# Attention's pieces planned with latencies that depend on the solve, and their end announced three jobs ahead

## The chip, the cores and the metric

One core of one Trainium2 chip runs the whole program. The metric is the device time of one execution in microseconds (us), the median over runs; for the kernel before it is 903.2 us over three runs (903.09 to 905.04).

## The reference

One layer of a hybrid block over 512 positions of 1024 channels, in fp32. After an RMSNorm, one projection `w_in` gives q, k, v of a stick-breaking attention, r, k, v and low-rank parts of an RWKV-7 branch, and two gates per channel:

```
h = rmsnorm(x, attn_norm_g);  proj = h @ w_in
# attention, 8 heads of 64, strictly causal, blocks of 128 queries
z = q @ k.T / 8;  keep = log_sigmoid(-z) where s < t else 0
w = exp(log_sigmoid(z) + sum of keep over s < j < t);  o_sb = w @ v
# RWKV-7, 8 heads of 64
S_t = S_(t-1) diag(w_t) + (S_(t-1) a_t) b_t^T + v_t k_t^T;  y_t = S_t r_t
o_rw = (groupnorm(y) + bonus) * gate
m = sigmoid(gate_0) * (o_sb @ w_branch_0) + sigmoid(gate_1) * (o_rw @ w_branch_1)
x = x + m @ w_out
u = causal_conv3(rmsnorm(x) @ w_ffn_up);  x = x + (silu(u_gate) * u_val) @ w_ffn_down
```

## The kernel before

Activations lie with channels on the 128 partitions and the 512 positions along the free axis. Every large product is made of three matmuls per 128 x 128 weight tile (weight high part times activation high and low part, weight low part times activation high part), so one output tile of `w_in` (8 weight tiles, called a dense tile here) is 24 matmuls of 512 columns. The weights of a tile come by a DMA on SP's queue (`load_w`, line 106, tile `wraw`, two buffers); ScalarE casts the high part (`whi`, line 108), and the low part (`wlo`) is made by ScalarE or VectorE with an accumulating DMA on POOL's queue (line 126).

After a short first stage the kernel has one long stage, which this change is about, and then the stages of the gates, `w_branch`, `w_out`, `w_up` and `w_down`, which run one dense product after another on TensorE (tiles `pf`, lines 138 to 140). In the long stage six streams of work are written as Python generators and merged by a planner, `interleave`, which runs when the program is built:

- `rw_stream(p)`, p = 0 to 3: RWKV for one pair of heads. Preparation, transposes and masked products (`st1`, lines 559 and 564), then the solve of small triangular systems: 31 steps of two VectorE operations (lines 595 and 597), whose result goes out and back through DRAM by DMAs on SP's queue (`su` and `st`, lines 602 and 604, then `U1` and `TT`, lines 608 and 611). The first matmul that reads it is line 618. After lines 629 to 649 comes a loop over 8 chunks (lines 666 to 691), the group norm and the output gate (line 715).
- `att_stream(p)`, the four chained: attention for one pair of heads, called a piece here. After the norms of q and k (lines 161 and 162) and the transposes of v (line 757) it has eight jobs, `(h, j)` with j from 3 down to 0 for each of two heads. A job works on n = 512 - 128 j columns: `scores` (TensorE lines 772 to 774 into a bank `pz`; then Abs, Exp, Ln on ScalarE, line 779 on VectorE, and the split into `sph`, `spl`; on POOL, lines 787 to 790, the running sum `ach`, `acl` that the next job reads), `weights` (lines 802 and 805 add onto the same `pz`, two Exps on ScalarE make `wth` and `w`, VectorE makes `wtl`) and `values` (lines 821 and 822). `pz` has two banks, so the scores of a job wait for the Exps of the job two before it.
- `dense_stream`: the dense tiles of q, k, v, r, k, v of all pairs (line 925, tiles `pd`) and, as filler, 13 of the 16 gate tiles (`NGATE`). Which tile comes next is decided in `pick`: r, k, v of the next RWKV pair first, then q, k, v of the next attention piece, each only once the event it hangs on (`prep`, `core`) is planned to come within `LAT["ahead"]` = 11059 ns; a gate tile otherwise.

Each stream yields its work in ns of TensorE time and its waits: `("lat", ns)` keeps it off the engine for so long, `("after", event)` until an event, `("set", event, ns)` announces one. The planner keeps a clock and takes at each point a stream that is ready. So the latencies, in the table `LAT`, set how far apart the steps of a stream stand in the instruction order; they wait for nothing on the chip. A piece is planned by `att0` and `att1`: job j may have its weights planned `att0[p] + att1[p] * (4 - j)` ns after its scores, and the event `core{p}`, on which q, k and v of the next piece hang, is set behind the piece's last values. The order of the instructions on the engines follows the planner, moved a little by the framework's own scheduling.

Where the long stage ends, TensorE goes on to three gate tiles, which need nothing of attention or RWKV (`pf`, first matmul line 138), and then to `w_branch`.

Of the kernel before, what the change touches and what calls it, by code (L numbers as in the profile page):

```python
# [52 lines left out]
def hybrid_block(ctx: ExitStack, tc: tile.TileContext, xT, w_in, vecs, decay_up, iclr_up, out_gate_up,  # L53
# [24 lines left out]
    def f(ap):  # L78
        return ap.bitcast(F32)
# [51 lines left out]
    def split(hi, lo, src):  # L131
        A.copy(hi, src)  # L132
        V.tensor_tensor(lo, src, f(hi), op=ALU.subtract)
# [20 lines left out]
    def f32r_pair(pool, tag):  # L154
        if tag == "wt":
            return tuple(pool.tile([P, T], F32R, tag=tag, name=tag + x, bufs=2) for x in "hl")
        return tuple(pool.tile([P, T], F32R, tag=tag + x, name=tag + x) for x in "hl")
# [26 lines left out]
    gl0 = f32r_pair(cpool, "gl0")  # L184
    gl1 = cpool.tile([96, T], F32R, name="gl1")
# [229 lines left out]
    def rbank():  # L415
        return bank(psr, "pr")
# [40 lines left out]
    def rw_stream(p):  # L457
        d = RD[p]
        yield ("after", f"prep{p - 1}")
        if p == 0:  # L460
            yield ("lat", LAT["rw0"][p])


        sic = []
        for j, bn in ((0, "db"), (1, "ib")):
# [11 lines left out]
            sic.append(e)  # L477
            yield (427, LAT["lup"][p] if j or p else 0)
        s, ic = sic
# [15 lines left out]
        V.tensor_tensor(sl, kk, f(sh), op=ALU.subtract)  # L495
        yield ("lat", LAT["sq"][p])
        pn = rbank()
# [39 lines left out]
        split(rh, rl, k)  # L537
        yield ("lat", LAT["prep"][p])
        pb = rbank()
# [10 lines left out]
        for hf in range(2):  # L550
            QA = rwp.tile([P, 4, 2, 256], F32, tag="QA", name="QA", bufs=4)
            QAs.append(QA)
            for c2 in range(2):
# [16 lines left out]
                for h in range(2):  # L570
                    A.copy(QA[:, 2 * c2 : 2 * c2 + 2, h].rearrange("p j (s n) -> p j s n", s=4)[:, :, 0:4:3],
                           pp[h][:, 256:512].rearrange("p (j s n) -> p j s n", j=2, s=2))
                yield (1400, LAT["st1"][p])
            for h, (hr, ho) in enumerate(HROWS):
# [17 lines left out]
        for q in range(31):  # L592
            n, m = 31 - q, q // 4 + 1
# [8 lines left out]
        nc.sync.dma_start(su.rearrange("b q (k g) t -> g (b q) k t", g=4), U)  # L602
        for g in range(4):
            nc.sync.dma_start(st[:, :, g], ut[32 * g : 32 * g + 16])
        yield ("lat", LAT["solve"][p])
        yield ("after", f"back{p - 1}")
        for h, (hr, _) in enumerate(HROWS):
# [115 lines left out]
    def att_stream(p):  # L723
# [42 lines left out]
        jobs = [(h, j) for h in range(2) for j in range(3, -1, -1)]  # L766
        st = {}

        def scores(h, j):
            n = T - P * j  # L770
            z = bank(psz, "pz")
            PE.matmul(z[:, 0:n], k2[h][:, j * P : (j + 1) * P], q2[h][:, j * P : T], start=True, stop=False)
            PE.matmul(z[:, 0:n], klo[h][:, j * P : (j + 1) * P], q2[h][:, j * P : T], start=False, stop=True)
            PE.matmul(z[:, 0:P], idb, mskb, start=False, stop=True, skip_group_check=True)
            e = atp.tile([P, T], F32, tag="e", name="e", bufs=3)
            act(e[:, 0:n], z[:, 0:n], AF.Abs)
            act(e[:, 0:n], e[:, 0:n], AF.Exp, scale=-1.0)
            act(e[:, 0:n], e[:, 0:n], AF.Ln, bias=1.0)
            V.scalar_tensor_tensor(e[:, 0:n], z[:, 0:n], 0.0, e[:, 0:n], op0=ALU.max, op1=ALU.add)
            sp = [atp.tile([P, n if j % 2 else T], F32R, tag=f"sp{x}{j if j % 2 else 0}", name=f"sp{x}{j}")[:, 0:n]  # L780
                  for x in "hl"]
            split(*sp, e[:, 0:n])

            if j == 3:
                ac = sp
            elif j > 0:
                G.tensor_tensor(e[:, P:n], e[:, P:n], st[h, j + 1]["e"][:, 0 : n - P], op=ALU.add)
                ac = [atp.tile([P, 3 * P], F32R, tag=f"ac{x}", name=f"ac{x}")[:, 0:n] for x in "hl"]
                G.tensor_copy(ac[0], e[:, 0:n])
                G.tensor_tensor(ac[1], e[:, 0:n], f(ac[0]), op=ALU.subtract)  # L790
            else:
                ac = None
            st[h, j] = dict(z=z, sp=sp, ac=ac, e=e)
            return n * 0.84 + 60

        def weights(h, j):
            n = T - P * j
            z, sp = st[h, j]["z"], st[h, j]["sp"]
            cost = 0
            if j < 3:  # L800
                for part in st[h, j + 1]["ac"]:
                    PE.matmul(z[:, P:n], none_, part, start=False, stop=True, skip_group_check=True)
                    cost += max(60, (n - P) * 0.42)
            for part in sp:
                PE.matmul(z[:, 0:n], ntri, part, start=False, stop=True, skip_group_check=True)  # L805
                cost += max(60, n * 0.42)
            w = atp.tile([P, T], F32, tag="e", name="w", bufs=3)
            wh, wl = f32r_pair(atp, "wt")
            act(wh[:, 0:n], z[:, 0:n], AF.Exp)
            act(w[:, 0:n], z[:, 0:n], AF.Exp)  # L810
            V.tensor_tensor(wl[:, 0:n], w[:, 0:n], f(wh[:, 0:n]), op=ALU.subtract)
            st[h, j]["w"] = wh, wl
            return cost

        def values(h, j):
            hr, ho = HROWS[h]
            n = T - P * j
            if j == 3:
                st[h, "po"] = bank(pso, "po")
            po, (wh, wl) = st[h, "po"], st[h, j]["w"]  # L820
            PE.matmul(po[:, j * P : T], vt[h][:, j], wh[:, 0:n], start=(j == 3), stop=False, skip_group_check=True)
            PE.matmul(po[:, j * P : T], vt[h][:, j], wl[:, 0:n], start=False, stop=(j == 0), skip_group_check=True)
            if j == 0:
                if h == 0:
                    st["ot"] = atp.tile([P, T], F32, tag="q0", name="ot")
                ot = st["ot"]
                A.copy(ot[hr], po[ho])
                V.tensor_tensor(ot[hr], ot[hr], po[hr], op=ALU.add)
            return 2 * n * 0.42

        def lat(j):
            return LAT["att0"][p] + LAT["att1"][p] * (4 - j)

        ready, free = {}, 0.0
        for i in range(-1, len(jobs)):
            if i + 1 < len(jobs):
                yield ("lat", max(0.0, free - clock["now"]))
                cost = scores(*jobs[i + 1])
                ready[i + 1] = clock["now"] + cost + lat(jobs[i + 1][1])
                yield (cost, 0)  # L840
            if i >= 0:
                yield ("lat", max(0.0, ready[i] - clock["now"]))
                cost = weights(*jobs[i])
                if i > 0:
                    cost += values(*jobs[i - 1])
                free = clock["now"] + cost + LAT["w"][p]
                yield (cost, 0)
        yield ("lat", LAT["val"][p])
        cost = values(*jobs[-1])
        A.dma_start(o_sb[p], st["ot"])  # L850
        yield ("set", f"core{p}")
        yield (cost, 0)

    clock = {"now": 0.0, "events": {f"{n}-1": 0.0 for n in ("prep", "core", "back")}}
    clock["events"]["back-2"] = 0.0
    gates = {}

# [16 lines left out]
    def dense_stream():  # L874
# [12 lines left out]
        def pick():  # L887
            for q in (rwq, atq):
                if q and all(ev.get(e, 1e12) <= clock["now"] + LAT["ahead"] for e in q[0][4]):
                    return q.pop(0)  # L890
            if gq and (rwq or atq or 16 - len(gq) < NGATE):
                return gq.pop(0)
# [12 lines left out]
        while cur:  # L905
# [14 lines left out]
            else:  # L920
# [10 lines left out]
            i += 1  # L931

    NGATE = 13
    FULL, SHORT = 0.65, 450
    LAT = dict(evac=5520, ahead=11059, k0=12000, gl0=1, gl1=2, att0=(1332, 762, 1125, 1575),
               att1=(810, 810, 810, 688), gn=(659, 3062, 2114, 3270), hop=(1073, 1254, 767, 762),
               lup=(8543, 2168, 5055, 862), pl=(671, 2115, 609, 2223), prep=(9000, 9000, 9000, 9000),
               pu=(1860, 2060, 1022, 1951), qk=(1409, 1644, 4330, 575), rw0=(5400, 1679, 2305, 1342),
               solve=(46500, 49755, 50000, 50000), sq=(2447, 1872, 3786, 557), sq_a=(1958, 1741, 1565, 328),
# [52 lines left out]
    def chain(*gens):  # L992
        for g in gens:
            yield from g

    interleave([rw_stream(p) for p in range(4)] + [chain(*(att_stream(p) for p in range(4))), dense_stream()])
    ph1.close()
    state["dma"] = False
# [147 lines left out]
```

## Time and profile before

| | us |
|---|---|
| median of 3 runs | 903.2 |
| the profiled execution, its own time | 898.13 |
| its span, first to last instruction | 896.4 |
| TensorE with matmuls, share of the span | 859.0 (96%) |
| VectorE, ScalarE, POOL busy | 562.5, 503.5, 148.1 |
| mean granted clock of TensorE | 0.987 |

The profile has one row per group of instructions with its busy time, and a trace of every instruction with start, duration and what released its engine after an idle time. The granted clock is 1.0 at TensorE's 2.4 GHz and 0.5 at 1.2 GHz. Ends of matmuls are modelled, so one matmul's duration is longer than the distance to the next.

### The profile page before, as it was taken

How to read it: one execution, taken by the hardware profiler on the slowest of the kernel's cores; microseconds unless marked ns; L12 is line 12 of the kernel's file. 1: busy time of each engine (PE TensorE's matmuls, PEld its weight loads, DVE VectorE, ACT ScalarE, POOL GpSimd, SP SyncE). 2: the span in 40 equal slices, each digit the busy share in tenths (PEclk: the TensorE clock that was granted, in tenths of full speed). 3: DMA queues.
4: the chain of work that ended last, by engine and by line, in shares of the span. 5: the costliest groups of instructions: out<-in, count | busy, mean ns of one | idle time of the engine just before them, and what ended most of it. 6: DMA issues, size and time to landing. Idle time of an engine off the chain costs nothing.

```text
span 896.4 us, 12726 instructions
## 1 busy us (share of the span) xinstructions
PE 859.0 (96%) x4598; PEld 676.7 (75%) x4598; DVE 562.5 (63%) x1138; ACT 503.5 (56%) x886; POOL 148.1 (17%) x214
## 2 busy tenths in 40 slices
PE   7889999988999989799999999999999999999998
PEld 4667767766777768586788878888888888888886
DVE  7669896894578681346666557777777777532222
ACT  7777988875766755677654454444444444321120
POOL 4633523251312523132000000000000000000000
PEclk9999999998899999899999999999999999999999
DMA  9476567338457548643664433333333333333431
GB/s 261 78 152 146 114 129 136 78 63 192 99 118 148 124 106 168 125 102 99 207 192 130 141 106 94 99 102 104 96 94 94 95 94 96 94 123 100 129 100 42
DMA packets 175151, 106.94 MB, mean 119 GB/s; under 512 B 29584, under 2 KB 156688, under 8 KB 175088
## 3 DMA queue, kind: packets, MB, share of 16 engines
q1 hardware_dynamic: 161408, 81.61, 32.3%
q0 software_dynamic: 10656, 19.40, 12.9%
q10 hardware_dynamic: 3024, 5.11, 1.6%
q8 instruction: 36, 0.59, 0.3%
q14 instruction: 27, 0.22, 0.1%
HBM read 78.31 MB, written 8.39 MB: 97 GB/s over the span
## 4 chain that ended last, share of the span: by engine, by line
PE 77%; DMA 7%; DVE 5%; ACT 5%; issue 2%; POOL 2%; SPq 1%; ACTq 0%; POOLq 0%; DVEq 0%
PE pf L138 17%; PE pf L139 17%; PE pf L140 17%; PE pd L925 13%; DMA wraw<-in_w_in 4%; PE pr L675 1%; PE pr L564 1%; DMA wlo<-wraw 1%; DMA U<-st 1%; PE pz L805 1%; DVE tm L595 1%; DVE U L597 1%; PE pr L559 1%; ACT whi L108 1%; PE pr L649 1%
## 5 line engine op out<-in xcount | busy, mean ns | idle before, releaser
L108 ACT CAST whi<-wraw 128x1024 fp32r<-128x1024 f32 (+1 forms) x131 | 129.1, 985 | 179.2 <-PE pf L139 146.9
L128 DVE TENSOR_TENSOR wlo<-wraw,whi 128x512 fp32r<-128x512 f32 (+1 forms) x178 | 114.4, 680 | 81.7 <-ACT whi L108 80.3
L138 PE MATMUL pf<-h2h,whi 128*128 128x512 f32 x352 | 137.3, 390 | 0.0
L139 PE MATMUL pf<-h2l,whi 128*128 128x512 f32 x352 | 136.9, 389 | 0.0
L140 PE MATMUL pf<-h2h,wlo 128*128 128x512 f32 x352 | 136.9, 389 | 0.0
L925 PE MATMUL pd<-hhi,whi 128*128 128x512 f32 x288 | 117.9, 409 | 0.0
L925 PE MATMUL pd<-hlo,whi 128*128 128x512 f32 x288 | 117.3, 407 | 0.0
L925 PE MATMUL pd<-hhi,wlo 128*128 128x512 f32 x288 | 85.4, 412 | 3.1 <-DMA wlo<-wraw 3.1
L126 POOL DMA_DIRECT2D wlo<-wraw x72 | 63.2, 936 | 142.7 <-ACT wlo L125 52.2
L139 PEld LDWEIGHTS pf<-h2l,whi 128*128 128x128 f32 x352 | 66.1, 188 | 13.9 <-issue 0.2
L138 PEld LDWEIGHTS pf<-h2h,whi 128*128 128x128 f32 x352 | 66.1, 188 | 13.9 <-issue 0.2
L140 PEld LDWEIGHTS pf<-h2h,wlo 128*128 128x128 f32 x352 | 66.1, 188 | 13.8
L140 PE MATMUL pf<-dh,wlo 128*128 128x512 f32 x176 | 69.3, 394 | 0.0
L138 PE MATMUL pf<-dh,whi 128*128 128x512 f32 x176 | 69.3, 394 | 0.0
L139 PE MATMUL pf<-dl,whi 128*128 128x512 f32 x176 | 69.3, 394 | 0.0
L925 PEld LDWEIGHTS pd<-hhi,wlo 128*128 128x128 f32 x288 | 52.5, 192 | 15.9 <-DMA wlo<-wraw 5.8
L925 PEld LDWEIGHTS pd<-hhi,whi 128*128 128x128 f32 x288 | 55.0, 191 | 11.0 <-ACT whi L108 0.2
L925 PEld LDWEIGHTS pd<-hlo,whi 128*128 128x128 f32 x288 | 54.8, 190 | 10.0
L1085 DVE TENSOR_TENSOR u<-pf,rs 128x512 f32<-128x512 f32 x44 | 30.3, 688 | 38.8 <-PE pf L140 38.7
L132 ACT CAST dh<-cv 128x512 fp32r<-128x512 f32 x22 | 13.6, 620 | 62.0 <-DVE cv L1094 62.0
L138 PEld LDWEIGHTS pf<-dh,whi 128*128 128x128 f32 x176 | 32.9, 187 | 8.3
L140 PEld LDWEIGHTS pf<-dh,wlo 128*128 128x128 f32 x176 | 32.9, 187 | 8.1
(324 smaller groups left out, 1691.0 us busy)
## 6 DMA issues: line engine op xcount, KB each, us to landing
wraw<-in_w_up SPq DMA_DIRECT2D x44, 512.0 KB, 3.6
wraw<-in_w_in SPq DMA_DIRECT2D x39, 512.0 KB, 3.9
wlo<-wraw POOLq DMA_DIRECT2D x72, 256.0 KB, 4.1
wraw<-in_w_down SPq DMA_DIRECT2D x16, 512.0 KB, 4.0
wraw<-in_w_branch SPq DMA_DIRECT2D x16, 256.0 KB, 2.8
wraw<-in_w_out SPq DMA_DIRECT2D x8, 512.0 KB, 3.8
gd<-gs ACTq DMA_DIRECT2D x13, 256.0 KB, 2.3
g<-gd SPq DMA_DIRECT2D x13, 256.0 KB, 3.1
```

Of the source, the lines that this page charges most:

```text
L108: after(A.copy(hi[:, 0:nk], raw[:, 0:nk]), state["last"])
L126: G.dma_start(lo[:, 0:n], raw[:, k0 : k0 + n], accum_op=ALU.add)
L128: V.tensor_tensor(lo[:, 0:n], raw[:, k0 : k0 + n], f(hi[:, k0 : k0 + n]), op=ALU.subtract)
L132: A.copy(hi, src)
L138: PE.matmul(ps, hi, ah, start=first, stop=False)
L139: PE.matmul(ps, hi, al, start=False, stop=False)
L140: PE.matmul(ps, lo, ah, start=False, stop=last)
L559: PE.transpose(pp[h][:, 256 + 128 * j + 64 * i : 320 + 128 * j + 64 * i], src.rearrange("p s t -> p (s t)"), ident[hr, hr])
L564: PE.matmul(pp[h][:, j * P : (j + 1) * P], BK[hr, ch].rearrange("p s t -> p (s t)"), ARV[hr, ch, 0 : 2 + h : 1 + h], start=True, stop=True)
L595: V.tensor_tensor(tv, U[:, 0:m, q : q + 1].broadcast_to([P, m, n]), N[:, q : q + 1, q + 1 :].broadcast_to([P, m, n]), op=ALU.mult)
L925: state["dense"] = PE.matmul(ps, w_, a, start=(n == 0), stop=(n == len(todo) - 1))
L1085: V.tensor_tensor(u, ps, rs2, op=ALU.mult)
```

## The change

Three edits, all to numbers and events of the planner. `rw_stream` notes, at the point where its solve is planned, the time until which the solve lasts. A piece's latency no longer depends on the pair but on whether a solve is planned to be under way when the scores are planned: 2500 + 1000 (4 - j) ns without one, 4300 + 1150 (4 - j) ns with one (before: 762 to 1575 + 688 to 810 (4 - j)). And `core{p}` is set when the weights of the job three before the last are planned, 11000 ns ahead, in place of at the piece's end. No instruction is added or taken away.

```diff
--- before.py
+++ after.py
@@ -602,6 +602,7 @@
         nc.sync.dma_start(su.rearrange("b q (k g) t -> g (b q) k t", g=4), U)
         for g in range(4):
             nc.sync.dma_start(st[:, :, g], ut[32 * g : 32 * g + 16])
+        clock["solve"] = clock["now"] + LAT["solve"][p]
         yield ("lat", LAT["solve"][p])
         yield ("after", f"back{p - 1}")
         for h, (hr, _) in enumerate(HROWS):
@@ -829,7 +830,9 @@
             return 2 * n * 0.42
 
         def lat(j):
-            return LAT["att0"][p] + LAT["att1"][p] * (4 - j)
+
+            s_ = clock["solve"] > clock["now"]
+            return LAT["att0"][s_] + LAT["att1"][s_] * (4 - j)
 
         ready, free = {}, 0.0
         for i in range(-1, len(jobs)):
@@ -845,13 +848,15 @@
                     cost += values(*jobs[i - 1])
                 free = clock["now"] + cost + LAT["w"][p]
                 yield (cost, 0)
+                if i == len(jobs) - 3:
+
+                    yield ("set", f"core{p}", CORE)
         yield ("lat", LAT["val"][p])
         cost = values(*jobs[-1])
         A.dma_start(o_sb[p], st["ot"])
-        yield ("set", f"core{p}")
         yield (cost, 0)
 
-    clock = {"now": 0.0, "events": {f"{n}-1": 0.0 for n in ("prep", "core", "back")}}
+    clock = {"now": 0.0, "solve": 0.0, "events": {f"{n}-1": 0.0 for n in ("prep", "core", "back")}}
     clock["events"]["back-2"] = 0.0
     gates = {}
 
@@ -931,9 +936,10 @@
             i += 1
 
     NGATE = 13
+    CORE = 11000
     FULL, SHORT = 0.65, 450
-    LAT = dict(evac=5520, ahead=11059, k0=12000, gl0=1, gl1=2, att0=(1332, 762, 1125, 1575),
-               att1=(810, 810, 810, 688), gn=(659, 3062, 2114, 3270), hop=(1073, 1254, 767, 762),
+    LAT = dict(evac=5520, ahead=11059, k0=12000, gl0=1, gl1=2, att0=(2500, 4300),
+               att1=(1000, 1150), gn=(659, 3062, 2114, 3270), hop=(1073, 1254, 767, 762),
                lup=(8543, 2168, 5055, 862), pl=(671, 2115, 609, 2223), prep=(9000, 9000, 9000, 9000),
                pu=(1860, 2060, 1022, 1951), qk=(1409, 1644, 4330, 575), rw0=(5400, 1679, 2305, 1342),
                solve=(46500, 49755, 50000, 50000), sq=(2447, 1872, 3786, 557), sq_a=(1958, 1741, 1565, 328),
```

What stands in another order now is shown at three places.

The first is TensorE's order at the end of the long stage: lines 772 to 774 (after: 773 to 775) are scores, 802 and 805 (803 and 806) weights, 821 and 822 (822 and 823) values, 925 (930) matmuls of a dense tile. Before, the last rows of piece 3:

```order
L925 MATMUL pd<-hhi,wlo 128x512 x5
L821 MATMUL po<-wth,vt 128x384
L802 MATMUL pz<-ach,none 128x384
L802 MATMUL pz<-acl,none 128x384
L822 MATMUL po<-wtl,vt 128x384
L925 MATMUL pd<-hhi,wlo 128x512
L805 MATMUL pz<-sph_4724,ntri 128x512
L925 MATMUL pd<-hhi,wlo 128x512 x2
L805 MATMUL pz<-spl_4725,ntri 128x512
L821 MATMUL po<-wth,vt 128x512
L138 MATMUL pf<-hhi,whi 128x512
```

and with the change, from the last dense matmuls of the stage on, which now stand ahead of piece 3's third job:

```order
L930 MATMUL pd<-hhi,wlo 128x512 x3
L773 MATMUL pz<-q_4320,k_4423 128x384
L774 MATMUL pz<-q_4320,klo_92 128x384
L775 LDWEIGHTS idb
L775 MATMUL pz<-mskb,idb 128x128
L803 MATMUL pz<-sph_4542,none 128x128
L803 MATMUL pz<-spl_4543,none 128x128
L806 MATMUL pz<-sph_4561,ntri 128x256
L806 MATMUL pz<-spl_4562,ntri 128x256
L822 MATMUL po<-wth,vt 128x128
L823 MATMUL po<-wtl,vt 128x128
L822 MATMUL po<-wth,vt 128x256
```

Before, matmuls of the last three dense tiles, of the RWKV chunk loop and of piece 3 alternate to the end. Now the last dense matmul of the stage stands ahead of the third of the eight jobs, and from there to `pf` there are only scores, weights and values. Between the scores of the first job and `pf` stand 15 dense matmuls and the four of line 716 (715 before).

The second place is SP's queue around the solve of pair 1: `sc` and `N` carry the solve's input, `su`, `st`, `TT` and `U` its result, `wraw` the weights of dense tiles. Before:

```order
L588 DMA N<-sc 32x1024 x4
L106 DMA wraw<-in_w_in 128x8x128 x3
L602 DMA su<-U 4x256x32
L604 DMA st<-N 512x1x8 x4
L611 DMA TT<-su 32x8x32 x3
L608 DMA U_98<-st 32x8x32 x2
L611 DMA TT<-su 32x8x32
L106 DMA wraw<-in_w_in 128x8x128 x2
```

and with the change:

```order
L588 DMA N<-sc 32x1024 x4
L106 DMA wraw<-in_w_in 128x8x128 x5
L602 DMA su<-U 4x256x32
L604 DMA st<-N 512x1x8 x4
L612 DMA TT<-su 32x8x32 x3
L609 DMA U_98<-st 32x8x32 x2
L612 DMA TT<-su 32x8x32
L577 DMA sc<-QA 32x4x32 x4
```

Five weight tiles instead of three are asked for between the solve's input and its result.

The third is the same queue around the solve of pair 2. Before there were five weight tiles in it:

```order
L588 DMA N<-sc 32x1024 x4
L106 DMA wraw<-in_w_in 128x8x128 x5
L602 DMA su<-U 4x256x32
L604 DMA st<-N 512x1x8 x4
L611 DMA TT<-su 32x8x32 x3
```

and with the change three, with a fourth behind `st`:

```order
L588 DMA N<-sc 32x1024 x4
L106 DMA wraw<-in_w_in 128x8x128 x3
L602 DMA su<-U 4x256x32
L604 DMA st<-N 512x1x8 x4
L106 DMA wraw<-in_w_in 128x8x128
L612 DMA TT<-su 32x8x32
```

On VectorE, the eight jobs of attention piece 1 stood among the 62 operations of pair 1's solve; now five of them stand between that solve and pair 2's, and three among pair 2's. Of piece 2, before, five jobs stood ahead of pair 3's solve and three among its operations; now four stand among them and four behind. Piece 0 keeps its place at pair 0's solve, and piece 3 stands behind all solves, before and now.

## Rows read from the trace of the kernel before

**Rows 1.** The page: span, TensorE's busy time, granted clock in 40 equal slices.
```profile
span 896.4 us, 12726 instructions
...
PE 859.0 (96%) x4598; PEld 676.7 (75%) x4598; DVE 562.5 (63%) x1138; ACT 503.5 (56%) x886; POOL 148.1 (17%) x214
...
PEclk9999999998899999899999999999999999999999
```

**Rows 2.** Busy time by stretch: us, PE PEld DVE ACT POOL, PEclk, DMA share.
```profile
60.00:422.20 362.20, 339.91 (x2382) 259.48 (x2381) 248.00 (x644) 268.55 (x570) 116.03 (x166) 0.97 0.56 120
382.90:422.20 39.30, 37.28 (x248) 28.78 (x248) 20.84 (x44) 30.04 (x76) 11.12 (x15) 1.00 0.34 82
```

**Rows 3.** What TensorE waited for: line, releaser, us in total, times, longest.
```profile
PE pr L649 <- ACT wlo L125: 5.1, 1, 5.1
...
PE pz L802 <- DVE tm L595: 2.3, 2, 1.4
...
PE pz L802 <- DVE e L779: 1.4, 3, 0.7
PE po L821 <- ACT wth L69: 0.9, 1, 0.9
```

**Rows 4.** Timeline of TensorE: start, duration, line, [idle before <- releaser].
```profile
215.73 0.73 PE L925 MATMUL pd<-hhi,wlo 128*128 128x512 f32 x2 [1.57 <-DMA wlo<-wraw]
...
218.77 0.96 PE L618 MATMUL pr<-U,QA 32*32 32x32 f32 x28 [1.68 <-DMA U<-st]
...
374.58 1.73 PE L649 MATMUL pr<-TT,QA 64*64 64x64 f32 x21 [5.06 <-ACT wlo L125]
```

**Rows 5.** Busy time by stretch, short ones around TensorE's idle times.
```profile
214.10:218.40 4.30, 1.42 (x7) 0.81 (x6) 0.41 (x2) 2.08 (x5) 1.23 (x2) 1.00 1.18 197
218.40:228.60 10.20, 9.83 (x72) 7.42 (x73) 5.28 (x9) 4.51 (x8) 3.14 (x4) 0.50 0.53 127
372.00:378.80 6.80, 4.22 (x37) 3.60 (x38) 4.34 (x7) 4.57 (x9) 1.71 (x2) 0.50 0.46 80
319.50:330.00 10.50, 8.43 (x62) 6.69 (x61) 9.07 (x33) 5.31 (x14) 1.69 (x3) 1.00 0.43 91
```

**Rows 6.** Timeline of TensorE, the last job of piece 3 to the first matmul behind the stage.
```profile
413.42 0.50 PE L772 MATMUL pz<-q,k 128*128 128x512 f32 x1
...
414.76 0.39 PE L925 MATMUL pd<-hlo,whi 128*128 128x512 f32 x1
414.99 0.39 PE L925 MATMUL pd<-hhi,whi 128*128 128x512 f32 x1
...
418.98 0.41 PE L802 MATMUL pz<-ach,none 128*128 128x384 f32 x1 [0.71 <-DVE e L779]
...
421.84 0.50 PE L821 MATMUL po<-wth,vt 128*128 128x512 f32 x1 [0.94 <-ACT wth L69]
422.18 0.39 PE L138 MATMUL pf<-hhi,whi 128*128 128x512 f32 x1
```

**Rows 7.** ScalarE's operations of a job by width: count, busy us, mean ns.
```profile
L69 ACT ACTIVATE e<-e 128x512 f32<-128x512 f32 x16 | 10.0, 627 | 0.1
...
L69 ACT ACTIVATE e<-e 128x384 f32<-128x384 f32 x16 | 8.4, 526 | 0.1
```

**Rows 8.** Timeline of SP's queue around the solves of pairs 1 and 2.
```profile
157.74 1.72 SPq L588 DMA_DIRECT2D N<-sc  x4
...
203.85 0.58 SPq L602 DMA_DIRECT2D su<-U  x1
...
217.22 3.33 SPq L106 DMA_DIRECT2D wraw<-in_w_in  x2
...
239.80 2.21 SPq L588 DMA_DIRECT2D N<-sc  x4
...
283.42 0.58 SPq L602 DMA_DIRECT2D su<-U  x1
```

**Rows 9.** Timeline of ScalarE ahead of line 649's wait.
```profile
368.54 1.05 ACT L108 CAST whi<-wraw 128x1024 fp32r<-128x1024 f32 x1 [4.45 <-DMA wraw<-in_w_in]
```

## The prediction

> **What bounds the kernel now.** I read the page first: TensorE has matmuls in flight for 96% of the span, and its granted clock is below 1.0 in a few slices only [rows 1]. So time is won or lost where TensorE stands idle or runs at the low clock, nowhere else. Then I cut the span into stages. From 60 to 422.2 us, the long stage that the planner orders, TensorE is idle for 362.2 - 339.9 = 22.3 us and its mean clock is 0.97 [rows 2]; behind 422.2 us the order of TensorE is the same in both programs. The change touches nothing but this stage, and adds no instruction, so it can win at most these 22.3 us and some low clock.
>
> The waits of TensorE tell where the 22.3 us lie [rows 3]: the largest one is 5.1 us, of line 649, and the waits of attention for its own latency, which the change is about, are 2.3 + 1.4 + 0.9 = 4.6 us. The reader should see that attention hardly waits as it is: its pieces are mixed so closely with dense tiles that the short planned latencies are mostly covered.
>
> Two idle places carry a second price. Behind 1.57 + 1.68 us of idle at 214 to 219 us [rows 4], TensorE ran for 10.2 us at clock 0.50, and around the 5.06 us at 369.5 us for 6.8 us [rows 4, 5]. At 0.50, the 1.2 GHz level, each busy us is worth half of one.
>
> **The end of the stage, the term that decides.** With the change the last dense matmul of the stage stands ahead of piece 3's third job, so TensorE has little to do beside the chain of the jobs. Its length goes like this. The last job, 512 columns wide, has its scores at 413.42 and its first value matmul at 421.84, and TensorE waited for that job twice in between [rows 6]: 8.4 us is the chain of one wide job, with three dense matmuls in it. A job that is 128 columns narrower saves about 0.1 us on each of its operations, as Exp on ScalarE does (627, then 526 ns) [rows 7]; with five ScalarE and two VectorE operations, and about six matmul passes of 0.06 us, that is 1.05 us. So the four jobs of a head take 8.4 + 7.3 + 6.3 + 5.2 = 27.2 us one after another; as there are two `pz` banks two jobs run side by side, and eight jobs take 2 x 27.2 / 2, about 27 us.
>
> What TensorE does in these 27 us: a job streams about 2n + 128 columns of scores, 4n - 256 of weights (2n where j is 3) and 2n of values, 19,456 columns for the eight; a 512-column matmul takes 0.23 us (414.76 to 414.99) [rows 6], so 8.7 us. The 15 dense matmuls and the four of line 716 behind the first scores add 19 x 0.23 = 4.4 us. Idle: 27 - 13.1 = 13.9 us. Before, the same eight jobs were spread over 39.3 us with dense work between them and TensorE idled 39.3 - 37.3 = 2.0 us [rows 2], of which 0.71 + 0.94 us stand at their very end [rows 6]. I count those 1.7 us as gone: the end costs **12.2 us** more idle time.
>
> Its clock is not in the trace, since no stretch before is so thin. Below: nothing, as behind the 2 us of idle at 319.9 us the clock stayed 1.00 [rows 5]. Above: all of attention's 8.7 us at half speed, of which half lies on the path as two jobs share the engine, 4.3 us, and 10.2 us of low clock in the dense work behind, as at 218.4 us, 5.1 us: 9.4 us. The nearest row is the stretch from 372 us, where 4.2 busy us at 0.50 cost 2.1 [rows 5]; I take that behind the end, and 2 us within it, **4 us**. The end costs 16.2 us together.
>
> The Trainium skill (TensorE: Matmul & The Clock Gate, Part 1) has a rule against this change: idle gaps between bursts of matmuls bring the array back to the half clock, and each burst after them starts slow. The trace agrees at 218.4 and 372 us [rows 5] and differs at 319.5 us, where 2 us of idle left the clock at 1.00 [rows 5]. By the rule alone the end would cost its upper bound; that is a rival below.
>
> **What is won earlier.** (a) Pair 1's solve. Piece 1's jobs shared VectorE with it, and its input and result lie 203.85 - 157.74 = 46.1 us apart on SP's queue; pair 2's, without attention, 283.42 - 239.80 = 43.6 us [rows 8]. Behind it stand the waits of 1.57 us, for a weight tile that is asked for behind the solve's result at 217.22 [rows 8], and 1.68 us for the result itself [rows 4]. With the change five weight tiles are in front of the result and no attention lies in the solve, so I take both as gone: 2.9 us of idle from 214.1 to 218.4 and half of 10.2 us at clock 0.50 [rows 5], **8.0 us**. (b) The 5.06 us at line 649. There ScalarE's in-order queue was held by a cast whose weights came 4.45 us late [rows 9]; behind the cast stood the split of q, whose VectorE part stood in turn ahead of the copy that line 649 reads. With the change dense tiles are spread wider there and the split comes behind; but casts of weights still stand in ScalarE's queue between copies that RWKV waits for. All of it would be 5.1 + 2.1 = 7.2 us [rows 4, 5], none of it 0; I take half, **3.6 us**. (c) Of attention's waits, the 2.3 us on VectorE's solve [rows 3] go, as longer latencies are planned there: **2.3 us**. Sum: 13.9 us.
>
> **What is lost earlier.** Pair 2's solve now holds three jobs of piece 1, and has three weight tiles between input and result where it had five: what pair 1 had. At least nothing, if the dense work placed before its result covers it; at most pair 1's 8.0 us; 46.1 - 43.6 = 2.5 us is what attention adds to a solve with eight jobs in it [rows 8]. I take **2 us**. The early event `core` brings no q, k, v tile earlier than before, because the pieces end later: it only keeps the delay from growing. The later places of q, k and v trade with gate tiles, and 13 gate tiles stay 13: nothing on TensorE.
>
> **Sum.** 16.2 + 2 - 13.9 = +4.3 us. The profiled execution took 898.13 us, 1.7 more than its span of 896.4 [rows 1]; it would become 902.4. Against the median of 903.2, five above that execution, I give 907.5 us.
>
> **Rivals.** First, faster: the waits at pair 1's read-back and at line 649 both go with their low clocks (8.0 + 7.2 + 2.3 = 17.5 us), pair 2's solve stays covered, and the clock holds through the end. Then 12.2 - 17.5 = -5.3, 898 us. It is decided by line 649's wait: with the end at 12.2, anything over that won earlier is a gain. For it: each of these waits hung on the very neighbours that the change moves apart. Against it: it needs a full clock in a stretch with TensorE busy less than half the time.
>
> Second, much slower: the clock falls in the thin end and stays down behind it, and pair 2's solve inherits pair 1's wait: 12.2 + 9.4 + 8.0 - 13.9 = +15.7, 919 us. For it: two of the three idle places shown in [rows 5] were followed by 0.50. Against it: pair 2's solve has fewer jobs in it than pair 1's had.
>
> Third, no change: the end costs 12.2 to 14 us and the waits earlier give back as much, 903 us. It is the case between forecast and first rival, if (b) is won whole and the clock costs about nothing.
>
> **How the numbers follow.** Forecast (end 16, two thirds won back) 0.39, second rival 0.24, first 0.25, third 0.12. A measurement of this kernel can tell about 0.2%, 1.8 us, from no change. So slower 0.63, same 0.12, faster 0.25. The forecast's own range is 905 to 913. For 8 in 10 I go to 895, the first rival with 3 us more of the 22.3 won, and to 922, the second with 3 us more of line 649's wait left.
>
> **What would show it.** Right: the profile after has pair 1's read-back (lines 609 and 619) without idle; the last 25 us before the first `pf` matmul have TensorE busy under 60%, with waits of lines 803, 806 and 822 on ScalarE and VectorE summing to over 10 us where they were 1.7; the first `pf` matmul stands near 427 us instead of 422.18 [rows 6]; behind it all rows repeat. Wrong: an idle sum in the end under 8 us (then the chain is shorter than 8.4 us per wide job without dense matmuls in it); a first `pf` ahead of 420 us (then the earlier waits weighed more); or a granted clock of 0.5 for over 20 us around the end.

## The result and the profile after

With the change the kernel takes 897.75 us (median of 4 runs, 895.15 to 897.9) against 903.17 us (903.09 to 905.04): a ratio of 0.9928, 95% interval 0.9906 to 0.995. It is faster by 0.7%, where 0.5% slower was forecast; the time lies inside the range. Yet the two profiled executions hardly differ: 897.9 us after, 898.13 before. Both facts have to be explained. Three executions in the record, of 1330 to 1766 us, are left out of every median and ratio here.

The page of the changed kernel has the same span as before [rows 1], at a lower clock near the twentieth slice:

```profile
span 896.2 us, 12738 instructions
...
PE 862.3 (96%) x4598; PEld 677.5 (76%) x4598; DVE 563.3 (63%) x1138; ACT 503.2 (56%) x886; POOL 147.2 (16%) x214
...
PEclk9998999999999999995999999999999999999999
```

Its busy times by stretch (columns as in [rows 2]): the long stage up to the first scores of piece 3, the end from there to the first `pf` matmuls, and three short stretches.

```profile
60.00:389.50 329.50, 317.07 (x2297) 242.48 (x2296) 233.59 (x615) 247.32 (x517) 107.22 (x154) 0.99 0.62 131
389.50:420.03 30.53, 24.29 (x89) 17.09 (x88) 15.41 (x30) 22.79 (x54) 7.98 (x12) 0.67 0.16 52
400.00:423.90 23.90, 19.31 (x52) 13.56 (x53) 9.91 (x18) 14.73 (x33) 5.33 (x8) 0.50 0.03 10
75.70:82.50 6.80, 6.80 (x29) 5.25 (x26) 2.90 (x7) 4.00 (x11) 1.21 (x2) 0.50 0.98 193
214.00:229.00 15.00, 14.66 (x203) 11.43 (x200) 10.53 (x21) 13.89 (x32) 8.96 (x15) 1.00 0.76 170
```

The same view of the kernel before, up to its first scores of piece 3 and in a stretch of low clock that the rows ahead of the prediction don't show:

```profile
60.00:382.90 322.90, 302.62 (x2135) 230.70 (x2134) 227.16 (x600) 238.51 (x495) 104.91 (x151) 0.97 0.59 125
136.40:139.80 3.40, 3.40 (x10) 2.65 (x10) 1.91 (x4) 2.14 (x5) 0.84 (x2) 0.51 0.84 180
```

I count as lost what TensorE is idle, and half of what it is busy at 0.50. Ahead of piece 3, before: 322.9 - 302.6 = 20.3 us of idle and half of 3.4 + 9.8 + 4.2 busy us ([rows 5] and the row above), together 29.0 us. After: 12.4 us of idle and half of 6.8, together 15.8 us. So 13.2 us were won there. At the end, before: 2.0 us [rows 2]. After: 6.2 us of idle and half of 19.3, 15.9 us. So 13.9 us were paid there. That the two sums nearly cancel is what the two equal spans say. The count takes in the clock, and that differs between executions (see the base runs); the idle time alone is 7.9 us less ahead of piece 3 and 4.2 us more at the end.

The waits of TensorE in the changed kernel, the same view as [rows 3]:

```profile
PE po L822 <- ACT wth L69: 5.4, 7, 1.5
...
PE po L823 <- DVE wtl L812: 1.7, 2, 0.9
PE pz L773 <- ACT w L69: 1.4, 4, 0.6
PE pr L162 <- DVE sll L701: 1.4, 1, 1.4
PE pr L619 <- DMA U<-st: 1.4, 2, 0.8
```

The 5.1 us of line 649 are gone, and so are the long waits on VectorE's solve; what stands in their place are waits of attention for its own Exps (lines 822, 823 and 773), 5.0 of these 8.5 us at the end and the rest in piece 0, and 1.4 us each of line 162 and of line 619, the read-back of pair 0. The timeline at the end:

```profile
389.54 0.23 PE L773 MATMUL pz<-q,k 128*128 128x128 f32 x1
...
397.68 0.50 PE L773 MATMUL pz<-q,k 128*128 128x512 f32 x1 [0.30 <-ACT w L69]
...
411.53 0.69 PE L773 MATMUL pz<-q,k 128*128 128x512 f32 x1
...
418.98 0.79 PE L822 MATMUL po<-wth,vt 128*128 128x512 f32 x1 [0.69 <-ACT wth L69]
419.57 0.63 PE L138 MATMUL pf<-hhi,whi 128*128 128x512 f32 x1
```

The eight jobs take 30.0 us from 389.54 to 419.57, the first `pf` matmul stands 2.6 us ahead of where it stood [rows 6]. The first `pf` matmul is 0.63 us long where it was 0.39 [rows 6]; by the row above the clock is 0.50 from 400 to 423.9 us.

SP's queue around the solves of pairs 1 and 2, as [rows 8]:

```profile
160.40 2.73 SPq L588 DMA_DIRECT2D N<-sc  x4
...
204.90 0.57 SPq L602 DMA_DIRECT2D su<-U  x1
...
224.97 1.71 SPq L588 DMA_DIRECT2D N<-sc  x4
...
264.78 0.56 SPq L602 DMA_DIRECT2D su<-U  x1
```

From input to result it is 44.5 us for pair 1 (46.1 before) and 39.8 us for pair 2 (43.6 before).

### The profile page after: what moved, and what is told of

The parts are those of the page before. It is cut to its first block, busy times and chain, and to the rows that moved or that the text cites. A ratio compares the mean times of both kernels' runs of the same rounds, so it can differ in the third digit from the quotient of the medians.

```text
span 896.2 us, 12738 instructions
## 1 busy us (share of the span) xinstructions
PE 862.3 (96%) x4598; PEld 677.5 (76%) x4598; DVE 563.3 (63%) x1138; ACT 503.2 (56%) x886; POOL 147.2 (16%) x214
## 4 chain that ended last, share of the span: by engine, by line
PE 73%; DVE 10%; DMA 7%; ACT 5%; issue 2%; POOL 1%; SPq 1%; ACTq 0%; POOLq 0%; DVEq 0%
PE pf L140 16%; PE pf L138 16%; PE pf L139 16%; PE pd L930 12%; DMA wraw<-in_w_in 2%; DMA g<-gd 2%; DVE U L597 1%; DVE tm L595 1%; PE pr L676 1%; ACT whi L108 1%; PE pz L806 1%; DMA wlo<-wraw 1%; PE pz L773 1%; PE pr L564 1%; PE pr L667 1%
## 5 line engine op out<-in xcount | busy, mean ns | idle before, releaser
L930 PE MATMUL pd<-hhi,wlo 128*128 128x512 f32 x288 | 82.1, 405 | 0.9 <-DMA wlo<-wraw 0.8
L139 PEld LDWEIGHTS pf<-h2l,whi 128*128 128x128 f32 x352 | 66.1, 188 | 13.9 <-issue 0.2
```

The costliest lines, as they stand in the source:

```text
L139: PE.matmul(ps, hi, al, start=False, stop=False)
L930: state["dense"] = PE.matmul(ps, w_, a, start=(n == 0), stop=(n == len(todo) - 1))
```

## The experiments

Ratios are to the kernel before, timed on the same chip in the same rounds, with 95% intervals. Twelve runs were made, two of them of the two kernels themselves. What is called lost is counted as above: TensorE's idle time and half of what it is busy at 0.50.

**The base: both kernels again.** No edit.

> The kernel before, unchanged, for a second profile. Its profiled execution took 898.13 us and its median is 903.2. If the profiled one was a lucky execution (fewer stretches at the 0.50 clock behind the same idle places), this profile shows about 903 us, the same order with the same idle of about 22 us in the long stage, and 10 us more at the low clock. If the two differ by something else (outside the program's span, or a transfer), span or idle time shows it. Ratio to the kernel before: 1.000.

Measured: 901.49 us (12 runs, 899.37 to 904.53), ratio 0.9966 (0.9947 to 0.9986). Its profiled execution took 901.08 us, with a span of 899.4 us, 3.0 more than the first profile. The long stage and its four stretches of low clock, by busy times:

```profile
60.00:425.00 365.00, 343.92 (x2387) 262.81 (x2386) 248.27 (x645) 269.47 (x571) 115.41 (x166) 0.96 0.57 119
67.40:70.80 3.40, 3.40 (x10) 2.65 (x9) 3.24 (x6) 0.49 (x1) 0.00 (x0) 0.50 0.60 159
135.70:142.50 6.80, 6.80 (x24) 4.91 (x23) 2.24 (x5) 4.13 (x9) 1.70 (x3) 0.50 0.62 131
221.00:231.20 10.20, 10.06 (x72) 7.65 (x73) 5.28 (x9) 4.26 (x8) 3.38 (x5) 0.50 0.54 126
374.60:381.40 6.80, 4.18 (x37) 3.56 (x38) 4.34 (x7) 4.62 (x9) 1.71 (x2) 0.50 0.46 80
```

The idle time is no longer than before, 21.1 us where the first profile had 22.3 [rows 2]. The low clock is: a stretch of 3.4 us behind the first idle place, where the first profile had none, and 6.8 us where it had 3.4. These two alone cost 3.4 us, and the span is 3.0 us longer. So the same program pays differently for the same idle places, and the profiled execution that the prediction was summed on, at 898.13 us, lies below every one of the timed runs of the kernel before (898.58 at least). The ratio of a kernel to itself came out 0.34% off with an interval that excludes 1, so a measurement of this kernel tells no less than a third of a per cent from no change, and not the 0.2% of the prediction. The 0.7% of the change is about twice that.

> The changed kernel, unchanged, as the base of the other runs on the same chip. Ratio to the kernel before about 0.993 (0.990 to 0.995); thin end with some 24 us at the 0.50 clock in every profile if that clock belongs to the end, and not to this one execution.

Measured: 899.32 us (7 runs, 893.51 to 900.69), ratio 0.992 (0.989 to 0.9949), the first result again. Its busy times up to piece 3, in the end, and in the stretches of low clock:

```profile
60.00:393.20 333.20, 321.19 (x2297) 245.86 (x2297) 233.56 (x615) 246.57 (x517) 108.59 (x154) 0.97 0.61 130
393.20:423.50 30.30, 24.06 (x88) 16.95 (x87) 15.16 (x30) 22.55 (x54) 7.97 (x12) 0.67 0.17 53
75.60:82.40 6.80, 6.80 (x30) 5.12 (x27) 3.72 (x9) 4.35 (x10) 1.72 (x2) 0.50 0.66 155
143.80:154.10 10.30, 10.30 (x44) 8.04 (x44) 5.74 (x11) 6.95 (x16) 6.02 (x13) 0.50 0.66 104
403.20:427.10 23.90, 18.95 (x51) 13.17 (x51) 9.88 (x18) 15.22 (x34) 5.78 (x9) 0.50 0.05 17
```

The idle time repeats, 12.0 us ahead of piece 3 and 6.2 at the end, and so do the 23.9 us at 0.50 in the end: that clock belongs to the thin end and not to one execution. The 10.3 us at 0.50 from 143.8 us on are not in the first profile: the changed kernel too pays differently from one execution to the next.

**One half of the change each.** First the latencies alone:

```diff
-                if i == len(jobs) - 3:
-                    yield ("set", f"core{p}", CORE)
...
+        yield ("set", f"core{p}")
```

> The new latencies alone, the event core at the piece's end as before. Theory 1 (the latencies win the waits ahead of the end, the early event only limits how late the pieces come): the pieces come later still, no dense matmul is left between the last eight jobs, the end costs 3 to 5 us more than in the change, and the waits ahead of it stay gone: 900 to 904 us. Theory 2 (the early event is what wins, the latencies cost): 908 us or more, with the waits at the solves' read-back still there.

Measured: 913.88 us, ratio 1.0101 (1.0072 to 1.013). Neither theory's number. Theory 1's mechanism holds for the read-back of pair 1, which has no wait, and for the end, at a larger price. It doesn't hold for the sum ahead of the end: other waits stand there (lines 773 and 676 below), and with 18.9 us of idle and half of 20.1 busy at 0.50 it comes to 29.0 us lost, as much as before the change. The first scores of piece 3 stand at 418.2 us, 29 us later than in the change, and all 16 gate tiles have been used as filler by then, since nothing else was left to pick. The eight jobs of the end in this run's busy times by stretch:

```profile
418.20:450.70 32.50, 23.66 (x68) 15.61 (x68) 14.47 (x29) 22.22 (x54) 7.62 (x12) 0.53 0.04 13
```

And among its waits of TensorE:

```profile
PE pf L138 <- ACT oh L132: 5.2, 1, 5.2
PE pz L773 <- ACT w L69: 4.6, 4, 3.1
...
PE pr L676 <- ACT QA L671: 3.0, 2, 2.7
```

TensorE is idle for 8.8 of the 32.5 us, at a mean clock of 0.53. With no gate tile behind the end, it also waits 5.2 us for attention's result to come back through DRAM.

Then the early event alone, with the old latencies (the table `LAT`, not shown, has its old values again):

```diff
-            s_ = clock["solve"] > clock["now"]
-            return LAT["att0"][s_] + LAT["att1"][s_] * (4 - j)
+            return LAT["att0"][p] + LAT["att1"][p] * (4 - j)
```

> The old latencies with the event core set three jobs ahead. Pieces end early, some 200 dense matmuls lie between the last job and the next stage, so nothing of a thin end. Theory 1: attention's jobs and their work on VectorE stay in the solves, and the waits there stay: about the time before, 899 to 905 us. Theory 2: the early event alone wins the change's gain and keeps it, as the end is covered: 885 to 893 us.

Measured: 919.3 us (4 runs, 917.92 to 921.64), ratio 1.0167 (1.0142 to 1.0191). Both theories missed. Here attention runs so far ahead that a piece lies in each solve, and RWKV is what is late at the end. In this run SP's queue shows pair 2's solve, from its input to its result:

```profile
245.40 2.06 SPq L588 DMA_DIRECT2D N<-sc  x4
...
298.13 0.57 SPq L602 DMA_DIRECT2D su<-U  x1
```

Its waits of TensorE hold two that neither kernel has:

```profile
PE pr L676 <- ACT QA L671: 4.6, 1, 4.6
PE pf L138 <- DVE rkb L717: 3.8, 1, 3.8
```

Pair 2's solve takes 52.7 us from input to result, 9 more than before and 13 more than in the change, and TensorE waits at the end for RWKV's chunk loop and its output. So each half alone loses; the event undoes what the longer latencies would delay, and the latencies hold attention back from where the event would bring it. What counts is where the pieces come to lie.

**The thin end, filled.** The change with all gate tiles in the long stage (`NGATE = 16`), and the kernel before with the same edit as control.

```diff
-NGATE = 13
+NGATE = 16
```

> The change with all 16 gate tiles in the long stage (13 before), so that the three gate tiles that now follow the thin end may be planned into it: 72 more dense matmuls lie between the last eight jobs. Theory A (the thin end costs what the trace of the change shows: some 15 us idle or at half clock that the order of the change had won ahead of it): most of it is won, 882 to 888 us, no stretch of 20 us at clock 0.50 near 400 us. Theory B (the thin end costs little, since the three gate tiles' own time is only moved): within 2 us of the change.

> The kernel before with all 16 gate tiles in the long stage, the control for the run with the change: its end had no hole to fill. Both theories: within 3 us of the kernel before, 899 to 906 us. If it gains 5 us or more, the gate tiles gain for another reason than the thin end.

Measured: the change with 16 gate tiles 894.7 us (5 runs, 889.85 to 895.98), ratio 0.9887 (0.9852 to 0.9921); the control 910.63 us, 1.0082 (1.0054 to 1.011), slower where no change was expected. The control shows a price that I had not counted: with no gate tile left behind the stage, TensorE waits 6.6 us for `oh` and runs 5.4 busy us at 0.50 behind it. The control's wait, and then TensorE's timeline of the change with 16 gate tiles, which pays it too (in brackets the wait ahead of the instruction):

```profile
PE pf L138 <- ACT oh L132: 6.6, 1, 6.6
```

```profile
429.38 0.79 PE L138 MATMUL pf<-oh,whi 128*128 128x512 f32 x1 [5.16 <-ACT oh L132]
```

Theory A's time was missed by some 7 us. The gain over the change itself, 3 to 5 us, lies within overlapping intervals and decides nothing; the control does. The same edit costs 7.5 us where there is no hole and gains where there is one, a difference of 0.0195 in the ratios, so theory B, that the end costs little, is out. The end of the eight jobs itself is filled:

```profile
388.30:424.20 35.90, 33.09 (x160) 25.74 (x158) 16.42 (x31) 29.25 (x64) 11.62 (x17) 0.98 0.55 140
```

**The latencies without the solve.** The short pair of numbers everywhere (shown; dots stand for the rest of the table), and the long pair everywhere, (4300, 4300) and (1150, 1150).

```diff
-    LAT = dict(... att0=(2500, 4300), att1=(1000, 1150), ...
+    LAT = dict(... att0=(2500, 2500), att1=(1000, 1000), ...
```

> The change with the short pair of latencies (2500 + 1000 per step) everywhere, the solve ignored. Theory A (what wins is that the pieces leave the solves' VectorE time, and any longer latency does that as long as the pieces do not bunch at the end): between the change and the kernel before, 895 to 903 us, with waits of lines 803 and 806 on VectorE inside the solves of 2 to 4 us more, and no thin end. Theory C (that latencies follow the solve is what matters): 903 us or more, with the waits at the read-back of the solves as in the kernel before.

> The change with the long pair of latencies (4300 + 1150 per step) everywhere. No dense matmul is left between the last eight jobs. Theory A: ahead of the end as good as the change, and the end 4 to 8 us longer: 901 to 906 us. Theory C: the same end, and more lost ahead of it: over 906 us.

Measured: 898.88 us, ratio 0.9945 (0.9915 to 0.9976), and 904.49 us, 1.0029 (0.9997 to 1.0061). Both times are as theory A has it, and the long pair's end loses 8.9 us of idle and half of 24.8 busy at 0.50, 21.3 us where the change's loses 15.9. The short pair is as fast as the change within the intervals, so nothing shows that the latencies must follow the solve. Its profile:

```profile
60.00:381.60 321.60, 300.37 (x2105) 228.39 (x2104) 225.33 (x597) 235.03 (x489) 102.88 (x149) 0.96 0.58 122
381.60:422.98 41.38, 41.10 (x281) 32.67 (x280) 20.75 (x48) 32.90 (x81) 12.83 (x17) 1.00 0.46 107
```

```profile
PE pr L619 <- DMA U<-st: 4.1, 1, 4.1
```

The end is full. Ahead of it the waits are not as theory A has it: 4.1 us for pair 0's read-back are theory C's sign, and the stretch loses 21.2 us of idle and half of 23.0 busy at 0.50, 32.7 us, more than before the change. This profiled execution, at 901.04 us, was the ninth of twelve; where the 0.5% of the median comes from it doesn't show. Nor did the pieces leave the solves: seven of piece 1's eight jobs stand among the operations of pair 1's solve, which takes 53.1 us from input to result, and yet TensorE waits at no read-back of that pair.

**Won ahead and not paid at the end.** The new latencies for pieces 0 and 1 alone, then for piece 0 alone; the old ones for the others:

```diff
+            if p > 1:
+                return (0, 762, 1125, 1575)[p] + (0, 810, 810, 688)[p] * (4 - j)
             s_ = clock["solve"] > clock["now"]
```

> The change with the new latencies for pieces 0 and 1 only, the old ones for pieces 2 and 3. On VectorE piece 1 stands behind pair 1's solve as in the change; at the end 66 dense matmuls lie between the last eight jobs, as before the change, and not 15. Theory A (the change wins some 14 us ahead of the end, above all by taking piece 1 out of pair 1's solve, and pays some 13 us for the thin end): won ahead and not paid, 884 to 891 us, no wait at pair 1's read-back, no 20 us at clock 0.50 near 400 us. Theory B (what is won ahead is only attention put off, and comes back with it): 896 to 902 us.

Measured: **886.91 us, ratio 0.9806 (0.9762 to 0.985)**, 1.9% faster than before and clear of the change's interval. Theory A's number. In the run with piece 0 alone the condition is `p > 0`. Busy times of the run with both pieces, up to piece 3, in the end, and in the two stretches of low clock ahead of it:

```profile
60.00:382.90 322.90, 304.03 (x2177) 231.38 (x2175) 228.29 (x603) 238.15 (x499) 105.16 (x153) 0.98 0.61 127
382.90:417.28 34.38, 33.91 (x213) 25.75 (x213) 18.14 (x41) 28.19 (x71) 10.88 (x15) 1.00 0.33 79
233.60:237.00 3.40, 3.40 (x11) 2.73 (x10) 2.16 (x6) 1.63 (x6) 1.47 (x2) 0.50 0.87 189
76.50:83.30 6.80, 6.80 (x24) 4.96 (x24) 3.42 (x8) 4.05 (x10) 1.72 (x2) 0.50 0.63 146
```

The end has 0.5 us of idle at full clock, and `pf` begins at 417.28 us although this profiled execution, at 892.97 us, was the slowest of the six. Pair 1's read-back doesn't stall. Ahead of the end it loses 18.9 us of idle and half of 10.2 busy at 0.50, 24.0 us: of the 13.2 us that the change won there this execution keeps 5.0, one new wait being 2.2 us of piece 1's scores. At the end it loses 0.5 us where the change loses 15.9. Its other five executions ran at a mean granted clock of 0.994 to 0.998 where this one has 0.992, so they lose less by the clock than the rows show. This kernel beats both, and it is the change with the latencies of pieces 2 and 3 taken back.

> The change with the new latencies for piece 0 only. That alone makes piece 1 stand behind pair 1's solve (six of its eight jobs) and leaves the end covered (66 dense matmuls, and 18 behind the last scores). Theory A: as the run with pieces 0 and 1, 884 to 892 us. Theory B: 896 to 902 us.

Measured: 896.05 us, ratio 0.9903 (0.9867 to 0.9938), 4 us above what theory A allowed. The end is full (35.2 of 36.2 us at 1.00), but ahead of it is a wait that I had not expected. In this run's waits of TensorE it is

```profile
PE pr L559 <- ACT sq L69: 4.7, 1, 4.7
```

and by busy times the stretch behind it is

```profile
279.30:293.00 13.70, 11.49 (x56) 8.47 (x57) 6.55 (x13) 7.15 (x15) 3.21 (x6) 0.50 0.59 122
```

That is 4.7 us of idle at pair 3's transposes, and 5.7 us by the low clock behind. It can't be put down as the 9 us between the two medians: the profiled executions of the two runs took the same time, 892.92 us here, the third fastest of nine, and 892.97 us there, the slowest of six. What parts them in a typical execution stays open.

**Attention back in the solve, the end covered.**

```diff
-                if i == len(jobs) - 3:
+                if i == len(jobs) - 4:
```

> The change with the event core set four jobs ahead of the last in place of three, still 11000 ns. That is enough to put piece 1 back among the operations of pair 1's solve (all but the last three jobs) and to cover the end with 66 dense matmuls, all latencies as in the change. Theory A: nothing won at pair 1, nothing paid at the end: the kernel before, 898 to 905 us, with the wait at line 619 for pair 1 and a stretch at clock 0.50 behind it. Theory B: attention comes earlier and the end is covered, 888 to 895 us.

Measured: 901.12 us, ratio 0.9973 (0.9945 to 1.0001), the time that theory A has. Pair 1's solve takes 49.9 us, and the low clock stands where it stood before the change. SP's queue in this run:

```profile
155.40 1.84 SPq L588 DMA_DIRECT2D N<-sc  x4
...
205.30 0.58 SPq L602 DMA_DIRECT2D su<-U  x1
```

Its busy times in the stretch behind the solve:

```profile
219.90:237.00 17.10, 17.10 (x88) 12.44 (x90) 6.76 (x13) 8.85 (x19) 4.89 (x9) 0.50 0.41 91
295.00:305.20 10.20, 6.13 (x30) 4.70 (x31) 2.58 (x7) 4.72 (x11) 2.54 (x4) 0.50 0.63 155
```

The wait itself was another than expected: 1.8 us of line 467 for ScalarE, not line 619 for the result. And the time has a second source, the lower row: behind a wait that neither kernel has,

```profile
PE pr L559 <- ACT QA L571: 5.3, 1, 5.3
```

TensorE runs at 0.50 again. That is 5.3 us of idle and 3.1 us by the clock at pair 3's transposes, 70 us behind pair 1's solve. So the run shows the low clock coming back behind pair 1's solve, and not that the rest of its loss is the kernel before's.

**One gate tile more.** As above, with `NGATE = 14` in the changed kernel.

> The change with 14 gate tiles in the long stage (13 before, 16 in an earlier run, which won 3 us and had a new wait of 5 us behind the stage for attention's result). 39 dense matmuls lie between the last eight jobs, 24 more than in the change, and two gate tiles are left to hide that result. Theory A: a third of the thin end covered, 4 to 6 us won against the change. Theory B: within 2 us of the change.

Measured: 895.75 us, ratio 0.9905 (0.9868 to 0.9942), 2 to 4 us under the change where theory A had 4 to 6. The end has 27.4 busy of 32.1 us at a mean clock of 0.83 (24.3 of 30.5 at 0.67 in the change), so part of it is filled, and `pf` waits for no result with two gate tiles left. But the interval overlaps the change's and this run alone decides nothing.

## Why the prediction was wrong, step by step

**What bounds the kernel** was right: the kernels differ by idle time and low clock of TensorE in the long stage.

**Two steps failed.** The forecast of 907.5 us was 4.3 us above the median before, and the measured 897.75 us is 5.4 below it. Of these 9.7 us, 4.5 are errors in the terms of the sum, and 5.2 come from carrying the sum from one execution over to a median: the median lay 5.1 us above the profiled execution before, and 0.15 us below it after.

**The end** was to cost 12.2 us of idle and 4 us by the clock, 16.2; it cost 13.9. That this is near is partly luck, two misses that cancel: 4.2 us more idle than before, 8.0 less than summed, and 9.7 us by the clock, 5.7 more than summed. The eight jobs took 30.0 us, of which 27 were summed and 2 given to the clock. The idle was over-sized because TensorE was to do its work of 13.1 us at full clock beside the chain; it was busy for 23.8 of the 30.0 us, most of them at 0.50. The chain was also taken too long: a wide job goes from its scores at 411.53 to its first value matmul at 418.98 us, 7.5 us even at 0.50, where 8.4 were read off [rows 6]. The Trainium skill (TensorE: Matmul & The Clock Gate, Part 1) has it that bursts of matmuls behind idle gaps start slow. Both profiles of the change agree, with 23.9 us at 0.50 in the end, though in the first of them no idle place in that stretch is longer than 0.7 us. The prediction's upper bound by the clock, 9.4 us, is near the 9.7 by luck as well: it had 4.3 us within the end and 5.1 behind, and there were 7.5 within and 2.2 behind.

**What is won earlier, (a)**: its size was right in the first profile. Pair 1's read-back runs with 14.66 busy of 15 us at clock 1.00. The run with the event four jobs ahead puts the jobs back, and 17.1 us at 0.50 stand there again. But the run with the short pair has those jobs in that solve too and no wait at its read-back, so that it is the jobs' leaving that frees the read-back, and not the dense work placed beside it, isn't shown.

**(b)**: undersized. I took half of 7.2 us; line 649 waits no more, all of it went.

**(c)**: right, the waits of 2.3 us on the solve are gone. Against them stand waits that were not foreseen: of piece 0's values, 1.5 and 0.9 us at most, and 1.4 us each of lines 162 and 619.

**What is lost at pair 2's solve**: wrong in sign. I charged 2 us; its solve became 3.8 us shorter although three jobs lie in it, and TensorE doesn't wait behind it. Ahead of the end the net was to be 11.9 us and was 13.2.

**The sum** against the profiled execution was to be +4.3 us; the spans say -0.2. That is 4.5 us of error in the terms: 2.3 at the end, 1.3 ahead of it, and the rest in what this count does not resolve. How much that can be, the second profiles tell: over the long stage they lose 33.3 us before and 36.3 with the change, yet their spans are 899.4 and 899.0 us.

**The second failed step** is the last one, "Against the median of 903.2, five above that execution, I give 907.5 us". It carried a difference over from one execution to a median as if the five us were a fixed offset. That execution, at 898.13 us, lies below all timed runs of the kernel before, and at a mean granted clock of 0.987 where all but two of those with a clock on record have 0.976 to 0.986; its second profile has no more idle, 3.4 us more by the clock, and a span 3.0 us longer. So about three of the five us are the price of stretches at 0.50 that the kernel before paid in one execution and not in the other. So the first pair of profiles sets the best execution of the kernel before beside a typical one of the changed kernel (897.9 us, median 897.75). The second pair sets a middling one, the fifth of twelve, beside the slowest of seven. Neither pair shows the gain that the medians show. The middling one beside the typical one does in part: spans of 899.4 and 896.2 us, and 33.3 and 31.7 us lost over the long stage. The gain isn't only a choice of executions: at the same mean granted clock, 0.980 to 0.982, 38 timed runs of the kernel before have a median of 903.5 us and 8 of the changed kernel one of 897.75. Both measured ratios are below 1 by more than the 0.34% by which the kernel before differs from itself. Which stretches at 0.50 make up the rest in a typical execution of the kernel before stays open, as no profile caught one at its median.

**The signs.** All three that the prediction named for being wrong are there: 6.2 us of idle in the end (under 8), the first `pf` at 419.57 us (ahead of 420), and 23.9 us at 0.50 (over 20). Of the signs of being right only the first came, pair 1's read-back. TensorE was busy for 75% of the last 25 us, not under 60%, and the waits of lines 803, 806 and 822 in the end sum to 5.0 us, not to over 10.

**The rivals.** The first named what happened ahead of the end, pair 1's read-back and line 649 both free, with their clock. It was wrong in holding that the clock must stay full at the end for that, and its 898 us hit the median by luck: its terms were 17.5 us won and 12.2 paid, counted 13.2 and 13.9. The third, as much paid as won, is what the two first profiles show; only the median is another.

That the price of the thin end is real and can be left out is shown by the run with pieces 0 and 1 alone: its end loses 0.5 us, and it is 11 to 12 us faster than the change. That all of the early gain can be kept at the same time isn't: its profiled execution keeps 5.0 of the 13.2 us. Which of the earlier places gave which part of the 13.2 us was read from the traces and not taken apart by a run of its own.

## What to carry to other kernels

Where a planner mixes a chain of short steps into a stream of dense work, ask first where the chain's end comes to lie relative to the end of the dense work: here the new latencies are worth 0.7% on all four pieces, with a bare end, and 1.9% on the first two alone, with a covered one. Keep filler for the last piece, and leave independent tiles behind it for the result's way back through memory: two were enough here, none cost 5.2 to 6.6 us, and one was not tried. And before summing on a profiled execution, compare its time and its stretches of low clock with the timed runs; if it lies below all of them, it leaves out a cost that the median pays.

## What was not expected of the hardware

Equal idle places did not have equal prices. Behind 3.3 us of idle between 63 and 75 us one profile of the kernel before ran on at 1.0; behind 1.9 us at the same place the other had 3.4 us at 0.50; and behind 3.6 us there the change had 6.8 us. And TensorE stayed at 0.50 for 23.9 us while it was busy for 19.3 of them, with no idle place longer than 0.7 us among them; that stretch ends at 423.9 us, within the unbroken matmuls of `pf`.
